# A planner's costs, and the order of weights, in a two-layer hybrid decoder trunk on one core

## The chip, the cores and the metric

The kernel runs on one core of a Trainium2 chip. The metric is the device time of one execution in microseconds. Before the change the median of three runs is 1481.27 us (1480.85 to 1481.48).

## What is computed

Two layers work on a sequence of 512 tokens of width 1024. All four branches of a layer read one projection of the same input; their gated outputs are projected, merged and projected again:

```python
for l in range(DEPTH):
    h = x @ w_in[l]
    (rw_p, rw_g, q_lat, kv_lat, k_pe, mla_g, conv_u, conv_g, xq, xg,
     merge) = jnp.split(h, SPLIT_POINTS, axis=-1)
    y_rwkv = _rwkv7_branch(rw_p, rw_g, ...)          # 8 heads x 64, delta-rule state, token by token
    y_mla = _mla_branch(q_lat, kv_lat, k_pe, mla_g, ...)   # causal softmax attention, 8 heads
    y_conv = _conformer_conv_branch(conv_u, conv_g, ...)   # val * sigmoid(glu), causal conv of width 31
    y_mem = _memory_xattn_branch(xq, xg, mem, ...)   # 4 heads into 256 memory tokens
    branches = jnp.stack([y_rwkv, y_mla, y_conv, y_mem], axis=2)
    proj = jnp.einsum('bsnc,ncd->bsnd', branches, w_o_branch[l])
    gates = jax.nn.sigmoid(merge.reshape(B, S, N_BRANCH, D) + b_gate[l])
    merged = jnp.sum(gates * proj, axis=2)
    out = merged @ w_out[l]
    x = _layer_norm(DEEPNORM_ALPHA * x + out, ln_g[l], ln_b[l])
```

## The kernel before

**Tiling.** The input is kept transposed (channels on partitions, 512 tokens along the row). Each f32 operand is split into two parts, `h` and `l` (ACT casts the first, DVE subtracts to get the second), and each product is three matmuls: `xl*wh`, `xh*wh`, `xh*wl`. A chunk of 128 output channels takes one weight DMA of 512 KB, the two halves of its split, and 24 matmuls of 512 columns. The names in the rows follow the work: `glu` and `val` are the convolution's chunks, `taps` its 31 multiply-adds on DVE (`cacc`), `mk` and `mv` the keys and values of the memory, `m` and `po` the merge gates and the output projections, `rg`, `mg`, `cg`, `xg` the gate paths. A last digit is the layer.

**Causal attention** (`pair_item`, L1492, and `mla_block`). Head pair, head and query block number a block: `ms013_0` are the scores of pair 0, head 1, block 3, layer 0. A block goes through PE (`ms`), DVE (mask and maximum `nmm`), ACT (exponential `mP` and its sum `smm`), DVE (reciprocal, scaling), PE (transposes `mt`) and ACT (copy `mPT`). At most three blocks are under way. When a pair's eight blocks are done, twenty matmuls (`mo`) make its output. `xhead` (L1265) does the same for the memory: `xs`, `xP`, `xt`, `xPTh`/`xPTl`, `xo`. `key_rotary` (L1373) turns the rotary part of the keys, and sends it by eight DMAs (`kTh`, `kTl`) to the partitions where the heads expect it.

**The recurrence** (`rwkv_unit`, L770) is done in chunks of 64 tokens, in units named layer, pair of head groups and half (`1_2_1` is the last). Its products are small: 64x64 tiles of PE. `bo`, `tk`, `w`, `yb` and `ty` are its bonus sums, transposes to tokens, state products, outputs and transposes back. `others` (L989) masks and copies two products out of one PSUM tile: `BP` on DVE, `RA` on ACT.

**The order.** All five engines run their instructions in program order. That order is made when the program is written, by a planner (`Plan`, L67). It keeps a clock for each engine and a time for each tile. `Engine.__getattr__` (L211) gives each ACT, DVE and POOL instruction a cost by its length, `start` adds latencies between engines (130 ns from one engine to another, 185 from PE, 220 to PE), and `run` (L149) takes the next step of whichever generator's time has come, or else the next matmul of the stream of weight items. `due` and `plan.t += ...` set back a generator's next step. `Space` (L242) hands out PSUM slots: three pools hold two, two and four banks. A weight item is picked when its condition holds, and its DMA is then put on SyncE's queue (SP), in the order in which items are picked; three weight slots (L30) hold what has been fetched. `conv_items` (L1235) has the conditions: `val0` may be picked once `L["glus"]` exceeds 0, and `glus` is counted in `glu`, when the projection has been computed.

All ACT, DVE and POOL instructions are recorded at L237, matmuls at L288, transposes at L293, DMAs at L300.

## Time and profile before

| | before |
|---|---|
| median of three runs | 1481.27 us |
| profiled execution | 1481.47 us |
| its span | 1479.7 us |
| granted TensorE clock | 0.999 |
| PE busy | 1465.4 us, 11751 matmuls |
| DVE busy | 1034.6 us |
| ACT busy | 682.7 us |
| POOL busy | 140.6 us |
| HBM traffic | 134.32 MB read, 5.77 MB written |

The profiled execution is longer than its span by 1.8 us, which lie before the first and after the last instruction. A busy time is the sum of an engine's instructions with overlaps counted once. A row of the timeline begins with the start and the length in microseconds, then has the engine, the line, the operation, the output and inputs, the shape and the count. What stands in brackets is idle time of the engine ahead of the row and what ended it.

### The profile page before, as it was taken

The numbers are of one execution on the slowest core, as the hardware profiler recorded it, in microseconds if no ns is written. First come the engines' busy times: TensorE is split into PE (matmuls) and PEld (weight loads), VectorE is DVE, ScalarE is ACT, GpSimd is POOL, SyncE is SP. The second block draws the span as 40 slices with busy tenths as digits, with TensorE's granted clock in tenths as the row PEclk, the third lists the DMA queues.
The fourth block names the chain that finished last, engine by engine and source line by source line (L and its number), as shares of the span: only waits on it lengthen the run. The fifth ranks groups of instructions, "written<-read, shape, count | busy, mean of one in ns | idle before, by whom it ended". The sixth has DMA issues, their size and how long they took to land.

```text
span 1479.7 us, 28903 instructions
## 1 busy us (share of the span) xinstructions
PE 1465.4 (99%) x11751; PEld 1230.6 (83%) x11751; DVE 1034.6 (70%) x2018; ACT 682.7 (46%) x1327; POOL 140.6 (10%) x329
## 2 busy tenths in 40 slices
PE   9999999999999999999999999999999999999997
PEld 8888888888888888888999888888888788888886
DVE  6799998765747575545564889987856475756747
ACT  5546653425354453443264466633454454444331
POOL 0000000030303020000010000000041103121002
PEclk9999999999999999999999999999999999999999
DMA  6444232232232323333353252433232323233522
GB/s 216 139 131 109 82 115 96 90 77 95 71 87 79 93 75 97 115 116 130 113 165 111 74 147 73 121 94 103 82 96 76 96 61 96 74 98 117 169 94 78
DMA packets 89157, 153.49 MB, mean 104 GB/s; under 512 B 41024, under 2 KB 47424, under 8 KB 89024
## 3 DMA queue, kind: packets, MB, share of 16 engines
q1 hardware_dynamic: 89024, 151.65, 34.1%
q8 instruction: 92, 1.51, 0.4%
q14 instruction: 41, 0.34, 0.1%
HBM read 134.32 MB, written 5.77 MB: 95 GB/s over the span
## 4 chain that ended last, share of the span: by engine, by line
PE 91%; DVE 3%; ACT 2%; DMA 2%; issue 0%; POOL 0%; SPq 0%; ACTq 0%; DVEq 0%; POOLq 0%
PE ps_m L288 24%; PE po L288 12%; PE ps_v L288 3%; PE ps_cg L288 3%; PE ps_rg L288 3%; PE ps_xg L288 3%; PE ps_k L288 3%; PE ps_mg L288 3%; PE ps_r L288 3%; PE ps_xq L288 3%; PE ps_val L288 3%; PE ps_glu L288 3%; PE pz L288 2%; PE ms L288 2%; PE x L288 2%; PE ps_mk L288 1%
## 5 line engine op out<-in xcount | busy, mean ns | idle before, releaser
L237 DVE SCALAR_TENSOR_TENSOR cacc<-hpad,prm,cacc 128x512 f32<-128x512 f32 x240 | 179.2, 749 | 4.0
L237 ACT ACTIVATE tm<-ps_m,prm 128x512 f32<-128x512 f32 x64 | 44.1, 689 | 151.4 <-PE ps_m L288 148.6
L237 DVE SCALAR_TENSOR_TENSOR mt<-tm,po 128x512 f32<-128x512 f32 x48 | 32.9, 686 | 85.9 <-PE po L288 85.8
L237 POOL TENSOR_TENSOR tmpW<-ZT,W 64x14 f32<-64x14 f32 (+6 forms) x112 | 42.7, 382 | 8.0
L237 ACT ACTIVATE mP<-ms,nmm 128x128 f32<-128x128 f32 (+3 forms) x64 | 33.8, 530 | 17.4 <-DVE nmm L237 11.4
L237 POOL TENSOR_TENSOR ZT<-ZT,tmpW 64x14 f32<-64x14 f32 (+6 forms) x112 | 39.6, 354 | 8.8
L237 POOL TENSOR_SCALAR ZT<-W 64x256 f32<-64x256 f32 x8 | 5.2, 649 | 368.3 <-DMA W<-scr 250.1
L237 DVE TENSOR_TENSOR merged<-merged,mt 128x512 f32<-128x512 f32 x48 | 33.4, 696 | 1.6
L237 ACT COPY mPT<-mt 128x128 f32<-128x128 f32 (+3 forms) x64 | 26.1, 428 | 17.0 <-PE mt L293 16.7
L237 POOL MEMSET D<- 128x8 f32 x8 | 0.9, 112 | 326.8 <-PE ms L288 310.1
L237 DVE CUSTOM_DVE_ANT_0 ms<-ms,causal 128x128 f32<-128x128 f32 (+3 forms) x64 | 31.0, 499 | 0.2
L293 PE MATMUL mt<-cst,mP 128*128 128x128 f32 x160 | 26.3, 274 | 1.5 <-DVE smx L237 1.0
L237 POOL TENSOR_SCALAR lrs<-lmv 128x1 f32<-128x1 f32 x8 | 4.0, 502 | 246.1 <-DVE lmv L237 241.1
L237 DVE TENSOR_SCALAR mP<-mP,smm 128x128 f32<-128x128 f32 (+3 forms) x64 | 24.8, 387 | 2.4
L237 DVE SCALAR_TENSOR_TENSOR merged<-tm,po 128x512 f32<-128x512 f32 x16 | 11.0, 687 | 21.5 <-PE po L288 21.5
L293 PEld LDWEIGHTS mt<-cst,mP 128*128 128x128 f32 x160 | 19.6, 140 | 7.2 <-ACT xP L237 1.4
L237 POOL TENSOR_SCALAR gr<-gm 128x8 f32<-128x8 f32 x8 | 1.6, 198 | 227.9 <-DVE gm L237 227.9
L237 ACT ACTIVATE yb<-yb,mr,gr 128x64 f32<-128x64 f32 x64 | 22.1, 430 | 1.1 <-DVE mr L237 1.1
L237 ACT ACTIVATE xP<-xs,nmx 128x256 f32<-128x256 f32 x32 | 15.2, 475 | 13.1 <-DVE nmx L237 8.1
L237 ACT ACTIVATE z<-z,lnb,lrs 128x256 f32<-128x256 f32 (+2 forms) x11 | 7.0, 666 | 30.7 <-DVE lnb L237 30.7
L288 PE MATMUL ms<-kTl,qT 96*128 96x128 f32 (+3 forms) x64 | 21.1, 330 | 0.0
L288 PE MATMUL ms<-kTh,qT 96*128 96x128 f32 (+3 forms) x64 | 20.6, 322 | 0.0
(3570 smaller groups left out, 5231.5 us busy)
## 6 DMA issues: line engine op xcount, KB each, us to landing
w<-in_w_ch_dram SPq DMA_DIRECT2D x146, 512.0 KB, 3.6
w<-in_w_o_dram SPq DMA_DIRECT2D x32, 512.0 KB, 3.5
w<-in_w_out_dram SPq DMA_DIRECT2D x16, 512.0 KB, 3.5
w<-in_w_lat_dram SPq DMA_DIRECT2D x15, 336.0 KB, 3.0
w<-in_w_mk_dram SPq DMA_DIRECT2D x8, 512.0 KB, 3.4
w<-in_w_mv_dram SPq DMA_DIRECT2D x8, 512.0 KB, 3.7
w<-in_w_qk_dram SPq DMA_DIRECT2D x8, 320.0 KB, 3.1
x<-in_xT_dram SPq DMA_DIRECT2D x8, 256.0 KB, 4.6
```

The source lines that it names most:

```text
L237: return self.plan.keep(f(*a, **k))
L288: plan.keep(nc.tensor.matmul(o, lhsT, rhs, start=start, stop=stop))
L293: plan.keep(nc.tensor.transpose(o, i, ident))
```

## The change

It changes costs and conditions of the planner, and with them the order; every engine has the same instructions as before.

- Tiles in PSUM of the tags `ps` and `pp` get an entry in `Plan.read`: a reader on another engine starts at least 130 ns after the last reader.
- An ACT instruction that also writes a sum (`accum_out`) costs 130 ns more, and a DVE reciprocal `90 + 4n` in place of `65 + 1.04n` (n is 1 to 8).
- `others` copies `RA` before `BP` if ACT's clock is behind DVE's.
- In layer 0 `glus` is counted when `glu` is picked, not when it has been computed; `val` can so be picked right behind it.
- The generator of the key transfers is set back by 4000 ns.

```diff
     def start(self, eng, outs, ins):
...
+        for n in ins:
+            t, e = self.read.get(n, (0.0, eng))
+            s = max(s, t + (130.0 if e != eng else 0.0))
...
     def end(self, eng, t, outs, ins):
...
+        for n in ins:
+            if n in self.read:
+                self.read[n] = t, eng
...
-                c = 65 + 0.83 * n + 120 * hasattr(k.get("scale"), "tensor") + 90 * hasattr(k.get("bias"), "tensor")
+                c = 65 + 0.83 * n + 120 * hasattr(k.get("scale"), "tensor") + 90 * hasattr(k.get("bias"), "tensor") + 130 * ("accum_out" in k)
...
+            elif name == "reciprocal":
+                c = 90 + 4 * n
...
+        if tag in ("ps", "pp"):
+            self.plan.read[t.tensor.name] = 0.0, ""
...
+                first = plan.clk["ACT"] < plan.clk["DVE"]
+                if first:
+                    right()
                 for s in SUB:
                     V.tensor_tensor(out=by2(BP[s])[:, :, :, 64:128], in0=y0[:, 0, s],
                                     in1=cc("minc").unsqueeze(1).unsqueeze(1).to_broadcast([128, 2, 2, 64]), op=ALU.mult)
-                for s in SUB:
-                    S.copy(by2(RA[s])[:, :, :, 64:128], y0[:, 1, s].rearrange("p h c w -> p c h w"))
+                if not first:
+                    right()
...
-                L["glus"] += 1
+                L["glus"] += l
...
+            def first():
+                if l == 0:
+                    L["glus"] += 1
+
+            ch_item(CH_U + 4 + i, f"glu{i}", glu, lambda: L["vals"] >= i - l and (i < 2 or L["taps"][i - 2] >= 20), first)
...
             plan.due(*kr)
+            plan.t += 4000.0
             yield
```

What this moves is seen in the order of the instructions. First SyncE's queue in layer 0, around the first key transfers; `w8` is glu0's weight in both. Before, `w9` and `w10` are mk0 and mk1, `w11` is val0, `w12` mk2:

```order
L300 DMA w8_464<-in_w_ch_dram 128x1024
L300 DMA w9_494<-in_w_mk_dram 128x1024
L300 DMA w10_537<-in_w_mk_dram 128x1024
L300 DMA kTh0_0_356<-krh_0_580 32x512
L300 DMA kTl0_0_357<-krl_0_581 32x512
L300 DMA w11_609<-in_w_ch_dram 128x1024
L300 DMA kTh1_0_358<-krh_0_580 32x512
```

With the change `w9` is val0, `w10` and `w11` are mk0 and mk1, `w12` is glu1:

```order
L311 DMA w8_464<-in_w_ch_dram 128x1024
L311 DMA w9_494<-in_w_ch_dram 128x1024
L311 DMA w10_537<-in_w_mk_dram 128x1024
L311 DMA w11_603<-in_w_mk_dram 128x1024
L311 DMA kTh0_0_356<-krh_0_583 32x512
L311 DMA kTl0_0_357<-krl_0_584 32x512
L311 DMA w12_649<-in_w_ch_dram 128x1024
```

val0's weight has moved from fourth to second place, and the first key transfers stand behind one more weight. On PE val0 follows glu0 with the change; before, it followed mk1.

Next PE and DVE in the first head pair of layer 0, from the scores ms100 to the first products of `mo0`. PE before:

```order
L288 MATMUL ms100_0_1521<-kTh2_0_360,qTl10_0_1207 128x128
L293 MATMUL mt003_0_1529<-cst_81,mP003_0_1479 128x128 x4
L288 MATMUL ps_val2_0_1390<-xl7_0_247,w27h_1345 128x512
L288 MATMUL ps_val2_0_1390<-xh7_0_246,w27h_1345 128x512
L288 MATMUL ps_val2_0_1390<-xh7_0_246,w27l_1346 128x512
L288 MATMUL ms110_0_1543<-kTl3_0_363,qT11_0_1208 128x128
L288 MATMUL ms110_0_1543<-kTh3_0_362,qT11_0_1208 128x128
L288 MATMUL ms110_0_1543<-kTh3_0_362,qTl11_0_1209 128x128
L293 MATMUL xt01_0_1531<-cst_81,xP00_0_1317 128x128 x2
L293 MATMUL xt01_0_1531<-cst_81,xP01_0_1421 128x128 x2
L293 MATMUL mt013_0_1565<-cst_81,mP013_0_1499 128x128 x4
L293 MATMUL mt100_0_1573<-cst_81,mP100_0_1538 128x128
```

PE with the change:

```order
L299 MATMUL ms100_0_1524<-kTh2_0_360,qTl10_0_1207 128x128
L304 MATMUL mt003_0_1529<-cst_81,mP003_0_1480 128x128 x4
L299 MATMUL ms110_0_1546<-kTl3_0_363,qT11_0_1208 128x128
L299 MATMUL ms110_0_1546<-kTh3_0_362,qT11_0_1208 128x128
L299 MATMUL ms110_0_1546<-kTh3_0_362,qTl11_0_1209 128x128
L304 MATMUL mt013_0_1557<-cst_81,mP013_0_1501 128x128 x4
L299 MATMUL ms101_0_1565<-kTl2_0_361,qT10_0_1206 128x256
L299 MATMUL ms101_0_1565<-kTh2_0_360,qT10_0_1206 128x256
L299 MATMUL ms101_0_1565<-kTh2_0_360,qTl10_0_1207 128x256
L304 MATMUL xt01_0_1544<-cst_81,xP00_0_1317 128x128 x2
L304 MATMUL xt01_0_1544<-cst_81,xP01_0_1424 128x128 x2
L299 MATMUL mo0_0_1247<-mPT000_0_1395,v0_0_928 64x128
```

The last three val2 matmuls stand ahead of ms100 now, xt01 stands behind mt013, and mt100 no longer follows mt013: its place is behind the twenty matmuls of `mo0`, which begin in the last row. DVE in the same blocks, from the reciprocal of block 003 to the scaling of block 013, before:

```order
L237 RECIPROCAL smm003_0_1481<-smm003_0_1481 128x1
L237 TENSOR_SCALAR mP003_0_1479<-mP003_0_1479,smm003_0_1481 128x512
L237 SCALAR_TENSOR_TENSOR cacc1_0_1050<-hpad1_113,prm0_227,cacc1_0_1050 128x512
L237 TENSOR_TENSOR xPTl00_0_1516<-xt00_0_1497,xPTh00_0_1515 128x512
L237 RECIPROCAL smm013_0_1501<-smm013_0_1501 128x1
L237 TENSOR_SCALAR mP013_0_1499<-mP013_0_1499,smm013_0_1501 128x512
```

and with the change:

```order
L246 RECIPROCAL smm003_0_1482<-smm003_0_1482 128x1
L246 TENSOR_SCALAR mP003_0_1480<-mP003_0_1480,smm003_0_1482 128x512
L246 SCALAR_TENSOR_TENSOR hpad0_112<-tglu2_0_1159,ps_val2_0_1388 128x512
L246 RECIPROCAL smm013_0_1503<-smm013_0_1503 128x1
L246 TENSOR_SCALAR mP013_0_1501<-mP013_0_1501,smm013_0_1503 128x512
```

Between the two scalings hpad0, which reads val2's PSUM tile, stands in place of a tap of the convolution and xPTl00.

Last PE in the second head pair of layer 0, ahead of mt113. Before:

```order
L288 MATMUL ps_xq2_0_1746<-xh3_0_193,w29l_1662 128x512
L288 MATMUL ps_xq2_0_1746<-xl4_0_211,w29h_1661 128x512
L288 MATMUL ps_xq2_0_1746<-xh4_0_210,w29h_1661 128x512
L288 MATMUL ps_xq2_0_1746<-xh4_0_210,w29l_1662 128x512
L293 MATMUL mt113_0_1833<-cst_81,mP113_0_1796 128x128 x4
L288 MATMUL ps_xq2_0_1746<-xl5_0_224,w29h_1661 128x512
```

With the change:

```order
L299 MATMUL ps_xq2_0_1783<-xh3_0_193,w29h_1645 128x512
L299 MATMUL ps_xq2_0_1783<-xh3_0_193,w29l_1646 128x512
L304 MATMUL mt103_0_1809<-cst_81,mP103_0_1752 128x128 x4
L299 MATMUL ps_xq2_0_1783<-xl4_0_211,w29h_1645 128x512
L299 MATMUL ps_xq2_0_1783<-xh4_0_210,w29h_1645 128x512
L299 MATMUL ps_xq2_0_1783<-xh4_0_210,w29l_1646 128x512
L304 MATMUL mt113_0_1828<-cst_81,mP113_0_1775 128x128 x4
L299 MATMUL ps_xq2_0_1783<-xl5_0_224,w29h_1645 128x512
```

Three more matmuls of xq2 and the transposes mt103 stand between the first twelve of xq2 and mt113. xq2 as a whole has moved too: before, its first three matmuls follow pk2; with the change mt102, ms103, mt112, ms113 and xs11 stand between pk2 and xq2.

In the last unit of layer 1 the state products w1 and w2 and the transposes ty_1_2_1 come later by six, nine and three matmuls of 512 columns, and the outputs yb follow the transposes ty_1_2_0 directly, where nine matmuls stood between. From the merge's po00 on, some 107 us before the end, PE's order is as before.

More of the change, by code (lines that the diff above doesn't have):

```diff
@@ L89, in __init__ @@
         self.slots = {}
+        self.read = {}
     def start(self, eng, outs, ins):
@@ L991, in others, with right @@
                 yield
+                def right():
+                    for s in SUB:
+                        S.copy(by2(RA[s])[:, :, :, 64:128], y0[:, 1, s].rearrange("p h c w -> p c h w"))
+                first = plan.clk["ACT"] < plan.clk["DVE"]
+                if first:
+                    right()
                 for s in SUB:
@@ L1247, in val @@
                 L["vals"] += 1
-            ch_item(CH_U + 4 + i, f"glu{i}", glu, lambda: L["vals"] >= i - l and (i < 2 or L["taps"][i - 2] >= 20))
+            def first():
+                if l == 0:
+                    L["glus"] += 1
+            ch_item(CH_U + 4 + i, f"glu{i}", glu, lambda: L["vals"] >= i - l and (i < 2 or L["taps"][i - 2] >= 20), first)
             ch_item(CH_U + i, f"val{i}", val, lambda: PRM[l] is not None and L["glus"] > i and (i < 2 or L["taps"][i - 2] == 30))
```

## The prediction

> **What bounds the kernel now.** First the page: the busy time of each engine, the clock granted to TensorE (PE) in forty slices, and the chain that ended last.

> ```profile
> PE 1465.4 (99%) x11751; PEld 1230.6 (83%) x11751; DVE 1034.6 (70%) x2018; ACT 682.7 (46%) x1327; POOL 140.6 (10%) x329
> PEclk9999999999999999999999999999999999999999
> PE 91%; DVE 3%; ACT 2%; DMA 2%; issue 0%; POOL 0%; SPq 0%; ACTq 0%; DVEq 0%; POOLq 0%
> ```

> PE is busy 99% of the span at full clock, and nine tenths of the chain is PE itself. A change that only reorders the same instructions can therefore win no more than PE's waits, and lose only by making new ones. So I next asked for busy time by stretch. The columns are the stretch and its length, then the busy time of PE, weight loads, DVE, ACT and POOL.

> ```profile
> 40.00:200.00 160.00, 157.38 (x939) 133.89 (x938) 142.82 (x304) 90.48 (x201) 2.07 (x3) 1.00 0.43 122
> 200.00:1440.00 1240.00, 1239.08 (x10428) 1034.85 (x10427) 837.97 (x1589) 561.97 (x1067) 127.21 (x299) 1.00 0.33 99
> 1440.00:1480.00 40.00, 31.01 (x160) 26.48 (x158) 30.02 (x73) 6.29 (x12) 10.16 (x16) 0.95 0.23 79
> ```

> From 200 to 1440 us PE lacks 0.92 us of 1240. From 40 to 200 us (projections, softmax of both attentions) it lacks 2.62. The last 40 us lack 8.99, but there the order of PE is not changed. Next the list of PE's waits: who waited, for whom, total, times, longest.

> ```profile
> PE mt L293 <- DVE smx L237: 1.0, 1, 1.0
> PE w L288 <- ACT yc L237: 0.6, 1, 0.6
> PE mt L293 <- DVE mP L237: 0.5, 1, 0.5
> PE ps_val L288 <- DVE w11l L237: 0.5, 1, 0.5
> PE ps_xq L288 <- ACT xql L237: 0.4, 1, 0.4
> ```

> Each happens once, so each can be looked up. Busy time understates them, since a pipelined matmul's end is drawn into the wait. I therefore price a wait as the distance between two starts less the usual distance. Usual is 0.23 us for 512 columns, as the rows below show.

> **The change part by part.** Nothing is added or taken away on any engine, and the number of changes of PE's tile shape is the same. Every term is a wait that goes or comes.

> *Weights of val0.* The order on SyncE's queue changes, and val0's weights now come second instead of fourth. Starts on PE, then the queue:

> ```profile
> 41.38 0.28 PE L288 MATMUL ps_mk<-meml,w9h 128*128 128x256 f32 x1
> ...
> 47.33 0.29 PE L288 MATMUL ps_mk<-memh,w10h 128*128 128x256 f32 x1
> 47.46 0.28 PE L288 MATMUL ps_mk<-memh,w10l 128*128 128x256 f32 x1
> 47.90 0.50 PE L288 MATMUL ps_val<-xl,w11h 128*128 128x512 f32 x1 [0.17 <-ACT w11h L237]
> 48.24 0.40 PE L288 MATMUL ps_val<-xh,w11h 128*128 128x512 f32 x1
> 49.16 0.50 PE L288 MATMUL ps_val<-xh,w11l 128*128 128x512 f32 x1 [0.53 <-DVE w11l L237]
> ```

> ```profile
> 26.97 6.67 SPq L300 DMA_DIRECT2D w<-in_w_mk_dram  x2
> 42.40 0.53 SPq L300 DMA_DIRECT2D w<-in_w_ch_dram  x1
> ```

> From 47.46 to 47.90 is 0.44 where 0.13 is usual (47.33 to 47.46): 0.31 lost. From 48.24 to 49.16 is 0.92 for 0.23: 0.69 lost. Both wait for the two halves of w11, whose DMA was issued only at 42.40, behind two key transfers, which wait for the rotated key. In the new order val0 uses the weight issued second. That issue lies in the 26.97 row (two DMAs, over at 33.64), and val0 now stands where the 41.38 row has mk0, right behind glu0, so its weight has some 8 us to land and be split. Gain 1.00. The key transfers themselves move behind one more weight and land in the same few microseconds. I cost them at nothing: all of val0, mk0 and mk1, 24 matmuls each, stand ahead of the first scores, which read the keys. Without that cover the price would again be at most the 1.00.

> *mt100, mt013.* Each of the 64 causal score blocks goes PE ms, DVE max, ACT exponential with its sum, DVE reciprocal and scaling, PE transposes mt. The planner now reckons 130 ns more for the sum and more for the reciprocal, so it sets other work between.

> ```profile
> 131.38 0.62 PE L293 MATMUL xt<-cst,xP 128*128 128x128 f32 x4
> 131.84 0.60 PE L293 MATMUL mt<-cst,mP 128*128 128x128 f32 x4
> 132.97 0.30 PE L293 MATMUL mt<-cst,mP 128*128 128x128 f32 x1 [0.53 <-DVE mP L237]
> ```

> Four transposes take as long as xt01's four (131.38 to 131.84, 0.46), but mt100 starts 1.13 after mt013: 0.67 lost. Now mt100 stands behind all twenty matmuls of mo0. Gain 0.67. In exchange mt013 has lost distance to its own scores:

> ```profile
> 126.79 0.40 PE L288 MATMUL ms<-kTl,qT 96*128 96x512 f32 x1
> 127.49 0.40 PE L288 MATMUL ps_val<-xl,w27h 128*128 128x512 f32 x1
> 128.20 0.60 PE L293 MATMUL xt<-cst,xP 128*128 128x128 f32 x4
> 128.88 0.47 PE L288 MATMUL ps_val<-xl,w27h 128*128 128x512 f32 x1
> ```

> ```profile
> 130.73 0.15 DVE L237 RECIPROCAL smm<-smm 128x1 f32<-128x1 f32 x1
> 130.92 0.49 DVE L237 TENSOR_SCALAR mP<-mP,smm 128x512 f32<-128x512 f32 x1
> 131.53 0.68 DVE L237 SCALAR_TENSOR_TENSOR hpad<-tglu,ps_val 128x512 f32<-128x512 f32 x1
> ```

> From ms013 at 126.79 to mt013 at 131.84 were 5.05 us. Three val2 matmuls (127.49 to 128.20, 0.71) and xt01 (0.46) no longer stand between, so 3.88 are left. The scaling of mP013 ended at 130.92 + 0.49 = 131.41, 4.62 behind ms013. DVE's order between has changed too: a cacc and an xPTl are gone, and hpad0 stands there instead. It reads val2, whose last group starts now after ms013 (0.70), val2 (0.71), xt00 and mt012 (128.20 to 128.88, 0.68). It has three matmuls of 0.23, with the end of the last some 0.2 later: 2.98 behind ms013. With hpad0 (0.68), and 0.68 for reciprocal and scaling by the starts 130.73 and 130.92, mP013 is ready at 4.34. A new wait of about 0.5. Its bounds are 0, if DVE is ahead, and 4.62 - 3.88 = 0.74, if DVE does as before. I take 0.5, since hpad0's release is worked out from rows.

> *xq2 and mt113.*

> ```profile
> 144.03 0.39 PE L288 MATMUL pk<-lth,w28l 128*128 128x512 f32 x1
> 144.83 0.50 PE L288 MATMUL ps_xq<-xl,w29h 128*128 128x512 f32 x1 [0.41 <-ACT xql L237]
> ...
> 150.67 0.39 PE L288 MATMUL ps_xq<-xh,w29l 128*128 128x512 f32 x1
> 152.04 0.63 PE L293 MATMUL mt<-cst,mP 128*128 128x128 f32 x4 [0.98 <-DVE smx L237]
> ```

> xq2 starts 0.80 after the last pk2 matmul where 0.23 is usual: 0.57 lost to ACT's xql, which had to empty a PSUM tile. In the new order xq2 stands behind ms103, ms113, xs11 and two groups of transposes. The two scores alone are six matmuls of 0.23, 1.4 us. Gain 0.57. mt113 starts 1.37 after the matmul ahead of it: 1.14 lost. Three more matmuls of xq2 (0.69) and the four transposes of mt103 (0.46) now stand ahead of it behind ms113, 1.15 together. On DVE a split of w30 now precedes ms113's maximum instead of following it, while the queue ahead starts earlier. I take a gain of 1.04, with bounds 0 (the split is felt in full) and 1.14.

> *xq3 of layer 1.*

> ```profile
> 867.45 0.39 PE L288 MATMUL pk<-lth,w146l 128*128 128x512 f32 x1
> 867.96 0.50 PE L288 MATMUL ps_xq<-xl,w147h 128*128 128x512 f32 x1
> ```

> ```profile
> 866.34 0.62 ACT L237 CAST yxg0h<-xy 128x512 fp32r<-128x512 f32 x1
> ```

> The distance 0.51 is 0.28 over the usual; xq3 waits for ACT's xql. Of ACT's queue the cast of yxg0 shown is moved away from before it, and its 0.62 exceed the wait. Gain 0.28.

> *The rest.* The wait of w3 of unit 1_0_0 for yc (listed, 0.6) keeps its order and stays, and so does po13's for tm13. The earlier place of the RA copies on ACT, longer sums in the norms, and the later bonus and token steps of units 0_0_0, 1_0_0 and 1_2_0 touch steps for which PE does not wait in the list. They bring nothing, and cost nothing while rows from 200 us on lack 0.92 of 1240. But 32 causal and 16 memory softmax groups of layer 1 are shuffled as well. I set 0.3 us for new waits there, between 0 and 2 us: none, or four of the size that the list shows for mP (0.5); 0.3 is near the lower end, as no layer 1 softmax wait is among the listed ones.

> *The last unit.* The order of its state products changes: w1, w2, the transposes ty and the outputs yb are each later or next to each other.

> ```profile
> 1342.77 0.39 PE L288 MATMUL ps_rg<-xh,w214l 128*128 128x512 f32 x1
> 1343.09 0.45 PE L288 MATMUL w<-S,Gs 64*64 64x64 f32 x8
> 1343.47 0.50 PE L288 MATMUL ps_rg<-xl,w215h 128*128 128x512 f32 x1
> 1343.81 0.39 PE L288 MATMUL ps_rg<-xh,w215h 128*128 128x512 f32 x1
> ```

> The eight 64x64 products start 0.32 after the last 512-column matmul (0.23 usual), and the second matmul behind them 0.34 after the first: a detour to small tiles costs 0.09 + 0.11 = 0.20. [...] But w0, w1, w2 and yb are four detours in either order, so the order gives 0, and I take 0; with one saved, the sum would come out 0.2 lower. PE has no listed wait in this unit, so nothing is to be won by moving; to be lost is a wait for yb or ty, which have some tenths of a microsecond to spare.

> **Sum.** 1.00 + 0.67 + 0.57 + 1.04 + 0.28 = 3.56 goes, 0.5 + 0.3 = 0.8 comes: 2.8 us less. The profiled execution took 1481.47, 0.20 above the median of the runs shown (1481.27) and within their spread. 1481.47 - 2.8 = 1478.7, from the median 1478.5. I predict 1478.6.

> **Rivals.** *DVE keeps the gain.* Between 40 and 200 us DVE works 142.82 of 160, 89%, and nearly all removed waits lie there. If PE arrives earlier but DVE cannot, the next transposes wait instead. Against it: waits were single, and before each DVE had free time. From two fifths to all of the gain of 2.8 would come back: 1479.8 to 1481.5.

> *More goes.* No new wait at all, mt113 whole (0.1 more), and the list's wait of w3 and po13's shrink by some 0.9 because everything ahead shifts: 3.56 + 1.0 = 4.6, 1476.9. For it: the planner's costs come nearer to the rows. Against it: their order is unchanged.

> *Slower.* The planner believes softmax sums longer and so puts another 512-column DVE step (hpad0 above, 0.68) ahead of a reciprocal whose transposes come soon. That costs 0.5 at mt013. Repeated at more than 7 of the 64 blocks (3.56 / 0.5) the kernel is slower than before, at 14 by over 0.2%: with 16, 1481.47 - 3.56 + 8 = 1485.9. Against it: most mt groups stand as far behind their scores as before, or farther.

> *It does not do what it says.* In the last unit there is no wait to remove, and the same number of detours. If yb or ty then comes late by 0.5, the result is 1479.1, inside my forecast's range.

> **How the numbers follow.** The forecast (1477.8 to 1479.8, the last rival included) has 0.53, DVE keeps the gain 0.25, more goes 0.16, slower 0.06. About 0.2% (2.96 us) is what a measurement of this kernel can tell from no change, so the border is at 1478.3 below and 1484.2 above. The forecast lies across the lower one: 0.21 of its 0.53 falls below. Faster is 0.21 + 0.16 = 0.37; slower 0.05, of the 0.06; the rest, 0.58, is the same. Leaving out the slower case and the outer ends, the range is 1476.6 to 1481.4. Its lower end is 1481.27 less the 3.56, mt113's 0.1 and 1.0 of the waits that I let stand.

> **What would show it.** In the new list of PE's waits, ps_val, ps_xq and the smx wait of mt should be gone, and mt with mP should remain once, near 131 us, for hpad0. val0 should begin straight after glu0 near 41.4. The window 40 to 200 should lack about 0.6 in place of 2.62, and 200 to 1440 about 1. The clock row and the last 40 us should not move. I am wrong if several new mt waits stand in layer 1 (815 to 970 us), if val1 or mk1 now waits for a late weight, or if yb waits in the last unit.

## The result, and the profile after

| | before | after |
|---|---|---|
| median, 13 runs each on one chip | 1481.27 us (1480.61 to 1482.01) | 1477.88 us (1477.14 to 1478.25) |
| profiled execution | 1481.47 us | 1477.30 us |
| its span | 1479.7 us | 1475.5 us |

The ratio is 0.9977, with a 95% interval from 0.9968 to 0.9985: 3.39 us faster, where 2.8 were forecast. The predicted 1478.6 is 0.7 too high. Before's time beside each experiment is from the same chip as the experiment (1481.05 to 1481.29).

Lines have moved in the changed kernel: ACT, DVE and POOL record at L246 (L237 before), matmuls at L299 (L288), transposes at L304 (L293), DMAs at L311 (L300). The page after, busy time, granted clock and the head of the chain:

```profile
PE 1464.9 (99%) x11751; PEld 1232.1 (84%) x11751; DVE 1034.8 (70%) x2018; ACT 681.8 (46%) x1327; POOL 144.8 (10%) x329
PEclk9999999999999999999999999999999999999999
PE 96%; DVE 1%; ACT 1%; POOL 0%; issue 0%; POOLq 0%
```

Work and clock are the same, and PE's share of the chain has risen from 91% to 96%: what has gone is waiting. By stretch (stretch, length, then busy time of PE, weight loads, DVE, ACT, POOL):

```profile
0.00:40.00 40.00, 38.74 (x231) 36.73 (x232) 24.20 (x54) 24.45 (x54) 1.15 (x11) 1.00 0.65 214
40.00:200.00 160.00, 159.57 (x956) 136.97 (x955) 145.10 (x312) 91.25 (x201) 2.06 (x3) 1.00 0.44 120
200.00:1440.00 1240.00, 1239.68 (x10427) 1035.36 (x10426) 837.18 (x1583) 560.10 (x1064) 131.43 (x299) 1.00 0.33 99
1440.00:1475.50 35.50, 26.89 (x142) 23.07 (x140) 28.34 (x70) 5.98 (x11) 10.15 (x16) 0.94 0.20 71
```

and the first stretch of before:

```profile
0.00:40.00 40.00, 37.90 (x229) 35.40 (x230) 23.79 (x54) 23.91 (x51) 1.16 (x11) 1.00 0.61 201
```

From 40 to 200 us PE now lacks 0.43 (2.62 before; some 0.6 was forecast), from 200 to 1440 us 0.32 (0.92; about 1 was forecast). The end is unchanged: before, the 39.7 us to the span's end lacked 8.69, now the 35.5 us lack 8.61. The first 40 us lack 0.84 less, but that isn't the change's: up to glu0 at 35 us PE's order is that of before, and in the executions below PE waits near 7 us between nothing and 1.05 us for the casts of its first input, and up to 0.4 for glu0 at 35 us. Without it the profiled executions differ by 4.17 - 0.84 = 3.3 us, close to the medians' 3.39.

The list of PE's waits after the change, whole (who waited, for whom, total, times, longest):

```profile
PE warm L299 <- POOL reset L246: 1.3, 1, 1.3
PE mt L304 <- ACT mPT L246: 0.4, 1, 0.4
PE po L299 <- ACT tm L246: 0.2, 1, 0.2
```

Of the five waits that the prediction quoted none is left under its name; one wait of mt is there, with ACT's copy named as what ended it. `warm` is ahead of the first product, in both kernels.

### The profile page after: what moved, and what is told of

Same layout as the page of the kernel before. It is cut to its first block, busy times and chain, and to the rows that moved or that the text cites. A ratio compares the mean times of both kernels' runs of the same rounds, so it can differ in the third digit from the quotient of the medians.

```text
span 1475.5 us, 28902 instructions
## 1 busy us (share of the span) xinstructions
PE 1464.9 (99%) x11751; PEld 1232.1 (84%) x11751; DVE 1034.8 (70%) x2018; ACT 681.8 (46%) x1327; POOL 144.8 (10%) x329
## 4 chain that ended last, share of the span: by engine, by line
PE 96%; DVE 1%; ACT 1%; POOL 0%; issue 0%; POOLq 0%
PE ps_m L299 24%; PE po L299 12%; PE ps_v L299 3%; PE ps_cg L299 3%; PE ps_rg L299 3%; PE ps_xg L299 3%; PE ps_xq L299 3%; PE ps_mg L299 3%; PE ps_k L299 3%; PE ps_val L299 3%; PE ps_glu L299 3%; PE ps_r L299 3%; PE pz L299 2%; PE ms L299 2%; PE pl L299 2%; PE x L299 2%
## 5 line engine op out<-in xcount | busy, mean ns | idle before, releaser
L246 DVE SCALAR_TENSOR_TENSOR cacc<-hpad,prm,cacc 128x512 f32<-128x512 f32 x240 | 179.1, 749 | 3.9
L246 ACT ACTIVATE tm<-ps_m,prm 128x512 f32<-128x512 f32 x64 | 44.1, 688 | 149.6 <-PE ps_m L299 146.9
L246 DVE SCALAR_TENSOR_TENSOR mt<-tm,po 128x512 f32<-128x512 f32 x48 | 33.0, 687 | 91.3 <-PE po L299 91.3
L246 POOL TENSOR_TENSOR tmpW<-ZT,W 64x14 f32<-64x14 f32 (+6 forms) x112 | 43.4, 388 | 8.0
L246 ACT ACTIVATE mP<-ms,nmm 128x128 f32<-128x128 f32 (+3 forms) x64 | 33.7, 529 | 20.6 <-DVE nmm L246 15.7
L246 POOL TENSOR_TENSOR ZT<-ZT,tmpW 64x14 f32<-64x14 f32 (+6 forms) x112 | 39.8, 355 | 8.8
L246 POOL TENSOR_SCALAR ZT<-W 64x256 f32<-64x256 f32 x8 | 4.7, 587 | 361.5 <-DMA W<-scr 361.5
L246 DVE TENSOR_TENSOR merged<-merged,mt 128x512 f32<-128x512 f32 x48 | 33.3, 694 | 1.6
L246 POOL MEMSET D<- 128x8 f32 x8 | 0.9, 111 | 329.6 <-PE ms L299 313.7
L246 DVE CUSTOM_DVE_ANT_0 ms<-ms,causal 128x128 f32<-128x128 f32 (+3 forms) x64 | 31.2, 499 | 0.6 <-PE ms L299 0.3
L246 ACT COPY mPT<-mt 128x128 f32<-128x128 f32 (+3 forms) x64 | 26.4, 428 | 5.3 <-PE mt L304 5.0
L246 POOL TENSOR_SCALAR lrs<-lmv 128x1 f32<-128x1 f32 x8 | 4.0, 501 | 244.7 <-DVE lmv L246 239.7
L304 PE MATMUL mt<-cst,mP 128*128 128x128 f32 x160 | 26.9, 274 | 0.4 <-ACT mPT L246 0.4
L246 DVE TENSOR_SCALAR mP<-mP,smm 128x128 f32<-128x128 f32 (+3 forms) x64 | 24.8, 387 | 2.4
L246 DVE SCALAR_TENSOR_TENSOR merged<-tm,po 128x512 f32<-128x512 f32 x16 | 11.0, 687 | 22.0 <-PE po L299 19.9
L304 PEld LDWEIGHTS mt<-cst,mP 128*128 128x128 f32 x160 | 20.2, 140 | 6.8 <-issue 0.8
L246 POOL TENSOR_SCALAR gr<-gm 128x8 f32<-128x8 f32 x8 | 3.3, 409 | 225.7 <-DVE gm L246 225.7
L246 ACT ACTIVATE yb<-yb,mr,gr 128x64 f32<-128x64 f32 x64 | 22.1, 431 | 0.7 <-DVE mr L246 0.7
L299 PE MATMUL ms<-kTl,qT 96*128 96x128 f32 (+3 forms) x64 | 21.5, 337 | 0.0
L246 ACT ACTIVATE z<-z,lnb,lrs 128x256 f32<-128x256 f32 (+2 forms) x11 | 7.0, 666 | 30.6 <-DVE lnb L246 30.6
L299 PE MATMUL ms<-kTh,qTl 96*128 96x128 f32 (+3 forms) x64 | 20.6, 323 | 0.0
L299 PE MATMUL ms<-kTh,qT 96*128 96x128 f32 (+3 forms) x64 | 20.6, 322 | 0.0
```

Of the source, the lines that this page charges most:

```text
L246: return self.plan.keep(f(*a, **k))
L299: plan.keep(nc.tensor.matmul(o, lhsT, rhs, start=start, stop=stop))
L304: plan.keep(nc.tensor.transpose(o, i, ident))
```

## The experiments

The theory behind the prediction: the time is PE's work and its waits, each wait can be read from the order with the durations of before's trace, and the longer costs of sums and reciprocals are what moves the softmax steps to better places. The main rivals: DVE keeps the gain, and the costs do it by no truth of theirs. Waits in the text are start to start less the usual distance, as in the prediction; the lists show idle time, which is mostly shorter.

**val0 early, alone.** Before, with two parts of the change only:

```diff
-                L["glus"] += 1
+                L["glus"] += l
...
+            ch_item(CH_U + 4 + i, f"glu{i}", glu, lambda: L["vals"] >= i - l and (i < 2 or L["taps"][i - 2] >= 20), first)
...
+            plan.t += 4000.0
```

> The kernel before with only the count of glu at its picking and the set-back of the key transfers, no cost changed. Theory A (each wait is a price of its own, removed by its own part): the two waits for w11's halves go, 1.00 us, every other wait of before stays: about 1480.3 where before is 1481.3. Rival B (DVE keeps the gain): PE comes 1.0 us earlier to the softmax stretch and waits there longer, so mt100 and mt113 wait about 1.0 more together and the time stays within 0.2 of before.

Measured: 1479.66 us against 1481.05, ratio 0.9990 [0.9981, 0.9999]. The list of PE's waits:

```profile
PE mt L293 <- DVE smx L237: 1.0, 1, 1.0
PE mt L293 <- DVE mP L237: 0.6, 1, 0.6
PE w L288 <- ACT yc L237: 0.6, 1, 0.6
PE ps_xq L288 <- ACT xql L237: 0.4, 1, 0.4
```

The two waits for w11 (0.31 + 0.69) are gone, and all others stand as before. The gain of 1.4 us is the 1.00 within its interval. Theory A held; rival B, by which DVE takes the gain back, fell, since no wait grew by more than 0.05.

**The costs, alone.** Before, with the longer sum and reciprocal only:

```diff
+ 130 * ("accum_out" in k)
...
+            elif name == "reciprocal":
+                c = 90 + 4 * n
```

> The kernel before with only the longer costs of sums and reciprocals. Theory A (the softmax waits mt100 0.69, mt113 1.14 and the xq2 and xq3 waits 0.57 and 0.29 are there since the planner took softmax for shorter than it is): they go or shrink, w11's stay: 1478.6 to 1479.6. Rival C (the turn-taking moved them): all of them stay, within 0.5 of before.

Measured: 1488.07 us against 1481.05, ratio 1.0044 [1.0031, 1.0057]: slower by 7.0. The waits of mt113 (1.13) and xq2 (0.56) are still there, and new ones have come: 1.50 and 0.81 of mt near 130 us, two of some 0.5, and a large one in layer 1. PE and then DVE there:

```profile
893.32 0.79 PE L290 MATMUL ps_glu<-xh,w149l 128*128 128x512 f32 x1 [2.32 <-DVE w149l L239]
893.91 0.63 PE L290 MATMUL ps_glu<-xl,w149h 128*128 128x512 f32 x1
894.34 0.63 PE L290 MATMUL ps_glu<-xh,w149h 128*128 128x512 f32 x1
```

```profile
891.44 0.69 DVE L239 SCALAR_TENSOR_TENSOR xg<-txg,ps_xg 128x512 f32<-128x512 f32 x1 [1.58 <-ACT txg L239]
892.04 1.22 DVE L239 TENSOR_TENSOR w149l<-w,w149h 128x1024 fp32r<-128x1024 f32 x1
```

The split of w149 was ready to run (ACT's cast of w149h was over at 889.30), but in DVE's order it stands behind xg, which waits 1.58 for ACT. PE loses 2.48 and then runs at half pace: 0.43 between starts (893.91 to 894.34) where 0.23 is usual. What theory A expected of the costs fell, and C with it: by themselves they make the kernel slower, not faster.

**The turns, alone.** Before, with `Plan.read` only:

```diff
+            t, e = self.read.get(n, (0.0, eng))
+            s = max(s, t + (130.0 if e != eng else 0.0))
```

> The kernel before with only the rule that engines take turns on one PSUM tile. Theory A (the softmax waits hang on the costs): mt100, mt113 and w11's waits stay; the waits for ACT's copies and reads out of PSUM (xq2 0.57, xq3 0.29, w3 0.65) may go: 1479.8 to 1481. Rival C (the turn-taking moved the softmax): mt100 and mt113 go, 1479.0 or less.

Measured: 1484.02 us against 1481.05, ratio 1.0017 [1.0008, 1.0026]: slower by 3.0. Three of the list's rows:

```profile
PE ps_val L297 <- DVE w11l L244: 1.8, 1, 1.8
PE mt L302 <- DVE mP L244: 1.4, 1, 1.4
...
PE mt L302 <- DVE smm L244: 0.7, 1, 0.7
```

The waits of mt113, xq2 and xq3 are gone here, without any change of cost. But val0, still behind mk1, now waits longer for w11 (1.94), and two waits of mt (1.50 and 0.85) have come near 133 us; behind them the granted clock falls to a half for 3.4 us (last section). Neither theory held whole: mt113's wait went, as C has it, and the time rose.

**Without RA first.** After, with `RA` always copied behind `BP`:

```diff
-                first = plan.clk["ACT"] < plan.clk["DVE"]
-                if first:
-                    right()
...
-                if not first:
-                    right()
+                for s in SUB:
+                    S.copy(by2(RA[s])[:, :, :, 64:128], y0[:, 1, s].rearrange("p h c w -> p c h w"))
```

> The changed kernel with BP always ahead of RA, all else as changed; PE and DVE move in 28 and 3 places only, ACT in none. Theory D (w3's wait of 0.65 went because ACT copies RA ahead of DVE's BP, and so reaches yc0 earlier): it comes back, about 1478.5 where the changed kernel is 1477.9. Rival E (it went because PE and ACT meet differently there for other reasons): no wait at w3, 1477.9 within 0.3.

Measured: 1478.12 us, ratio 0.9979 [0.9970, 0.9988]; the change whole has 0.9977, so the times don't tell the two apart. The rows do. In unit 1_0_0 first before, ACT and then the state product w3 on PE:

```profile
1175.84 0.65 ACT L237 COPY RA<-x_1x 128x256 f32<-128x256 f32 x2 [3.70 <-DVE BP L237]
...
1177.32 0.79 ACT L237 ACTIVATE yc<-cb,prm 128x512 f32<-128x512 f32 x1
```

```profile
1178.16 0.45 PE L288 MATMUL w<-S,Gs 64*64 64x64 f32 x8 [0.57 <-ACT yc L237]
```

then after:

```profile
1168.35 0.70 ACT L246 COPY RA<-x_1x 128x256 f32<-128x256 f32 x2
1171.62 1.06 ACT L246 CAST w194h<-w 128x1024 fp32r<-128x1024 f32 x1 [2.58 <-DMA w<-in_w_o_dram]
1172.65 0.78 ACT L246 ACTIVATE yc<-cb,prm 128x512 f32<-128x512 f32 x1
```

```profile
1173.88 0.45 PE L299 MATMUL w<-S,Gs 64*64 64x64 f32 x8
```

and in the experiment:

```profile
1171.92 0.65 ACT L246 COPY RA<-x_1x 128x256 f32<-128x256 f32 x2 [3.69 <-DVE BP L246]
...
1173.40 0.79 ACT L246 ACTIVATE yc<-cb,prm 128x512 f32<-128x512 f32 x1
```

```profile
1174.24 0.45 PE L299 MATMUL w<-S,Gs 64*64 64x64 f32 x8 [0.76 <-ACT yc L246]
```

RA and BP come out of one PSUM tile, x_1x in the rows. In before RA is second: ACT stands idle for 3.70 us until DVE's BP is over (1175.75; RA starts at 1175.84), the cast and yc queue behind RA, and w3 waits for yc. After, RA is first: it starts at 1168.35 without a wait, the cast waits only for its weight (2.58), and w3 has no wait in the rows. Theory D held in the rows: with this edit alone taken out of the change, w3's wait is back. ACT's order is the same with the edit and without it; what the edit turns round is which of the two engines waits for the other. By the traces ACT's RA stands idle for BP eight times in before, 11.4 us together, and once after, for 0.4 us; DVE's BP stands idle for RA never in before, and three times after, 1.8 us together. Made on the kernel of before alone, the edit changes no instruction's place on any engine, but by the program ACT's RA would be ahead of BP in seven of the eight units. That kernel was not run, so what the edit is worth there is not shown. In before and in this run the second of the two reads starts 0.09 us after the end of the first, and being the second cost ACT 3.70 and 3.69 us; what makes it wait was not shown.

**Without the turns.** After, with `Plan.read` taken out (the lines of the third experiment removed).

> The changed kernel without the rule of turns on a PSUM tile; costs, val0 early and RA first stay. Theory F (the parts add up: what the turns alone took away, mt113 1.14, xq2 0.54 and xq3 0.28, comes back when they are taken out): those three waits stand in the list, about 1479.8. Rival G (the order of the crowded stretch is dealt anew by every change of a cost, so that parts do not add up): other waits than these three, the time anywhere from 1478 to 1486.

Measured: 1480.76 us against 1481.29, ratio 0.9996 [0.9987, 1.0005]. mt113 (1.14) and xq2 (0.54) wait as before, mt twice near 130 us (0.96 and 0.69), and tk at 1083.5 us (0.51). Three of these make one row of the list:

```profile
PE mt L295 <- DVE mP L239: 2.3, 3, 1.0
```

F held for two of its three waits (that of xq3 stayed away) and not for the rest: three others came, as G has it, and the time is 1.0 above F's.

**Without the costs.** After, with the old costs of sum and reciprocal.

> The changed kernel without the longer costs of sums and reciprocals; turns, val0 early and RA first stay. Theory F: what the turns alone showed without its waits for w11 (2.2) and w3 (0.9): the two mt waits near 133 us of 1.5 and 0.85 stay, about 1480.8. Rival G: other waits. A rival H (with val0 early the costs do nothing more): 1477.9, no mt wait.

Measured: 1479.34 us, ratio 0.9988 [0.9979, 0.9997]. The list:

```profile
PE mt L302 <- DVE smx L244: 1.0, 1, 1.0
...
PE mt L302 <- DVE mP L244: 0.6, 1, 0.6
PE ps_xq L297 <- ACT xql L244: 0.4, 1, 0.4
```

These are before's waits less those for w11 and w3, each at its old size: mt113 1.14, mt100 0.74, xq2 0.55, xq3 0.28. H fell, and the waits of mt that F has were not there; G's "other waits" is what is left. The turns, which alone took away mt113's, xq2's and xq3's waits, take away none of them here: the same edit, on an order that has val0 early and RA first, moves other instructions.

**val0 late.** After, with `glus` counted in `glu` again and without the 4000 ns.

> The changed kernel without val0 early and without the set-back of the key transfers; turns, costs and RA first stay. Theory F: w11's waits of 1.0 come back and nothing else, about 1478.9. Rival G: mt and ps_val waits in layer 0 of another size, 1480 or more.

Measured: 1487.64 us against 1481.29, ratio 1.0040 [1.0027, 1.0053]: 9.8 us above the change whole, where only 1.3 hangs on w11l itself. Three of its rows:

```profile
PE ps_glu L299 <- DVE w149l L246: 2.3, 1, 2.3
PE xt L304 <- DVE xP L246: 1.9, 1, 1.9
...
PE ps_val L299 <- DVE w11l L246: 1.1, 1, 1.1
```

F fell, and the time is as G has it, but the two largest waits are not those that G named: 2.09 of xt at 170.75 us, and 2.48 of glu in layer 1. An edit at 40 us deals the order anew up to 895 us, where DVE's w149l is late again as in the run with the costs alone.

**The costs as the rows have them.** In the change's trace the read of a sum takes ACT 0.19 to 0.23 us and the reciprocal DVE 0.16. If better costs made the better order, these should be no worse than 130 and 94:

```diff
-  ... + 130 * ("accum_out" in k)
+  ... + 200 * ("accum_out" in k)
...
-                c = 90 + 4 * n
+                c = 155 + 1.04 * n
```

> The changed kernel with a sum at 200 ns more (in place of 130) and a reciprocal at 156 ns, as the rows of the trace have them. Theory I (nearer costs make fewer waits): the wait of mt013 (0.60) goes too and none comes, 1477.3 or less. Rival G (every change of a cost deals the order anew): new waits, 1479 to 1485.

Measured: 1490.56 us, ratio 1.0061 [1.0048, 1.0073], the second slowest of all. PE waits 3.70 for a key transfer of layer 1, 1.78 and 0.93 for w22 near 95 us:

```profile
872.73 0.44 PE L299 MATMUL ms<-kTl,qT 96*128 96x128 f32 x1 [3.54 <-DMA kTl<-xkl]
```

I fell. New waits came, as G has it, but the time is 5.6 above G's upper end.

This settles less than it seems to, for 200 and 156 ns are lengths of instructions, and the planner's other costs are nearer to the distance from one start to the next: a cast of 1024 columns costs 915 ns in the planner, takes 1044 ns in the rows of the change, and stands 945 ns ahead of the next start (medians). By that measure a sum costs 0.09 us (its read starts at 128.27, the next instruction at 128.36; 92 ns is the median of 72), and the reciprocal 0.19 (129.62 to 129.81 below). A sum near 92 ns together with a reciprocal near 190 was not tried.

**hpad0 later.** After, with hpad0 of val2 (layer 0) put off by 600 ns in the planner's time, so that it leaves the place ahead of mt013's scaling:

```diff
+                def put():
+                    plan.t += 600.0 if (l, i) == (0, 2) else 0.0
+                    if (l, i) == (0, 2):
+                        yield
                     V.scalar_tensor_tensor(out=hpad[:, 30:542], in0=d["t"], scalar=1.0, in1=ps, op0=ALU.add, op1=ALU.mult)
```

> The changed kernel with hpad0 of val2 in layer 0 put 600 ns later by the planner; on DVE it then stands behind the scaling of block 013, a tap of the convolution in its old place. Theory J (mt013 waits 0.60 since DVE does hpad0, which itself waits for val2, ahead of the scaling): the wait of mt013 is gone or under 0.2, 1477.3. Rival K (mt013 waits for ACT's copy to empty its PSUM tile, as the list names it): it stays at 0.5 or more, 1477.9.

Measured: 1477.56 us against 1481.14, ratio 0.9976 [0.9967, 0.9985]. First the change whole, PE (ms013, then mt013) and DVE:

```profile
125.95 0.40 PE L299 MATMUL ms<-kTl,qT 96*128 96x512 f32 x1
...
129.73 0.27 PE L299 MATMUL ms<-kTh,qTl 96*128 96x128 f32 x1
130.44 0.63 PE L304 MATMUL mt<-cst,mP 128*128 128x128 f32 x4 [0.43 <-ACT mPT L246]
```

```profile
129.01 0.69 DVE L246 SCALAR_TENSOR_TENSOR hpad<-tglu,ps_val 128x512 f32<-128x512 f32 x1 [0.82 <-PE ps_val L299]
129.62 0.16 DVE L246 RECIPROCAL smm<-smm 128x1 f32<-128x1 f32 x1
129.81 0.49 DVE L246 TENSOR_SCALAR mP<-mP,smm 128x512 f32<-128x512 f32 x1
```

then the experiment, PE (mt003 and mt013 in one row) and DVE:

```profile
129.09 1.13 PE L304 MATMUL mt<-cst,mP 128*128 128x128 f32 x8
```

```profile
128.96 0.49 DVE L246 TENSOR_SCALAR mP<-mP,smm 128x512 f32<-128x512 f32 x1
...
130.17 0.68 DVE L246 SCALAR_TENSOR_TENSOR hpad<-tglu,ps_val 128x512 f32<-128x512 f32 x1
```

With hpad0 behind the scaling, mt013 goes without a gap, though ACT's copy, which the list names, starts as late as it did (129.75): theory J, that DVE holds mt013, held. The time is that of the change all the same, for 0.89 came at tk, 1080 us, and 0.45 at pq, 138.5 us.

**Other costs of a sum.** The change with 150, 100 and 160 ns in place of 130:

> The changed kernel with the sum at 150 ns in place of 130: 62 places on PE move. Theory G (each deal of the order has its own waits, with no regard to which cost is nearer): one or two waits other than those of the changed kernel, 1477 to 1480. Theory I (nearer costs, fewer waits): 1477.9 or less.

> The changed kernel with the sum at 100 ns in place of 130 (387 places on PE move). Theory G: between 1477 and 1486, its waits in the stretches 100 to 200 or 800 to 1000 us. Theory I: slower by a little, mt113's wait partly back, 1478 to 1479.

> The changed kernel with the sum at 160 ns (1298 places on PE move). Theory G: like the measured costs, a large deal with a large wait somewhere, 1480 to 1490, its waits in the softmax stretches. Theory I: 1477.9 or less.

Measured, against 1481.14: 150 gives 1477.80, ratio 0.9978 [0.9969, 0.9987]; 100 gives 1482.35, 1.0010 [1.0001, 1.0019]; 160 gives 1491.23, 1.0069 [1.0056, 1.0081]. By PE's order 62, 387 and 1298 instructions stand elsewhere than in the change. With 160 the list begins:

```profile
PE po L299 <- DVE yrg2l L246: 3.1, 1, 3.1
...
PE x L299 <- ACT PT L246: 1.9, 1, 1.9
```

Ten nanoseconds more in a cost of the planner (160 against 150) make 13 us on the chip, where every engine does the same instructions. At 150 both theories have the time; at 100 and 160 I fell. G has the time at 100; at 160 it is 1.2 above G's, and the two largest waits lie at 1192 and 1383 us, outside the softmax stretches that G named. There is no slope toward either measure of a sum: 100, the nearest to 0.09 us, loses a little; 130 and 150 win; 160 and, with the longer reciprocal, 200 lose most.

## Why the prediction was right, and where it was not

**The sum did not add up by edit, but it did by wait.** Against before, val0 early alone gives -1.4 us, the costs +7.0 and the turns +3.0: +8.6 together, where the whole gives -3.4. RA first was not run alone; the 0.65 that the rows tie to it would not close that gap. Taken out of the whole, the turns are worth 2.9 us, the costs 1.5, val0 early 9.8 and RA first 0.2. The forecast came out because it priced no edit. It went through the order that the whole change makes and asked at each wait of before what stands there now.

- *val0, 1.00:* right. val0 starts straight behind glu0, at 41.13 (41.4 was forecast), and neither val1 nor mk1 waits for its weight. The experiment with this part alone shows it by itself.
- *mt100, 0.67, and xq2, 0.57:* right. Both waits are gone from rows and list.
- *mt113, 1.04:* gone whole, 1.14. It starts 0.24 behind the matmul ahead of it:

```profile
148.46 0.40 PE L299 MATMUL ps_xq<-xh,w29l 128*128 128x512 f32 x1
148.70 0.60 PE L304 MATMUL mt<-cst,mP 128*128 128x128 f32 x4
```

- *xq3 of layer 1, 0.28:* right; the list has it no more.
- *mt013, a new wait of 0.5:* right in place and cause, 0.60 in size. The working put the end of mP013's scaling 4.34 behind ms013; the rows above have 129.81 + 0.49 - 125.95 = 4.35. The wait is longer by the time from DVE's end to PE's start (130.30 to 130.44), which the working left out. The list's name for the releaser, ACT's mPT, was not the one that held it.
- *"The wait of w3 of unit 1_0_0 for yc ... keeps its order and stays":* **wrong**, and this is the step that failed. The order of ACT there has indeed not changed; the working took that to mean that the wait had not. But RA now runs ahead of BP instead of waiting for it, in several microseconds that were ACT's idle time, and no longer holds the cast and yc. It brought 0.65. "They bring nothing" was said of the RA copies in general; for this unit it was wrong. po13's wait, 0.36, did stay.
- *The rest, 0.3 for new waits in layer 1:* none came.
- *The last unit, 0:* right; no wait of ty or yb is listed, and the end lacks what it lacked.

Worked out anew with these sizes: 1.00 + 0.67 + 0.57 + 1.14 + 0.28 + 0.65 - 0.60 = 3.71 less. Medians say 3.39 with about 1.3 either way, and the profiled executions without the first 40 us 3.3; some 0.3 is smaller than what could be traced.

**The cause that the prediction gave for the softmax part fell.** It said that the planner reckons more for sum and reciprocal "so it sets other work between". The costs alone leave mt113 and xq2 waiting and add waits of 1.50 and 2.48 us; costs set to the lengths in the rows give the second slowest kernel; and turns without costs take the three waits away on the kernel of before, but not with val0 early and RA first. mt113 and xq2 wait together or not at all: both in each of the four kernels without the turns, neither in seven of the ten with them, both in the other three (no costs, a sum of 100, a sum of 160). So the turns were needed in all that was tried, and don't suffice. What is shown is that, among the combinations tried, mt113, xq2 and xq3 all lose their waits without a new one above 0.9 us only in this one and its near variants (without RA first, hpad0 later, a sum of 150). Why the planner arrives at it isn't a matter of one cost: each edit shifts its clocks, and every later choice follows. In before, and in the losing versions but for that with 160, most of the waiting lies in the two softmax stretches and the projections ahead of them (48 to 175 us, 870 to 900 us); in the first of these DVE too is busy most of the time, for 145.10 of the 160 us from 40 to 200 after the change.

**The slower rival** was put at 0.06, with hpad0-like steps repeated. In the change it did not happen. Its kind is not rare among the neighbours: of the eleven other versions that hold parts of the change or other sums, five were slower than before by over 0.15%, by late splits, key transfers and scalings: through a few waits of some 1.5 to 4 us rather than many of 0.5, and through the clock that fell behind them (last section). That second price stood nowhere in the prediction.

## What to carry to other kernels

Where a planner deals the order and the bound engine is 99% busy, price the order that comes out and not the edit that made it: list the few waits, and for each compare what stands between producer and consumer on both engines, before and after, the idle queue of the producer's engine included. Where two engines read one tile, look also at which waits for which: in unit 1_0_0 that turned round, and ACT's 3.70 us of standing idle for BP went, with ACT's order the same. Don't let waits pile up close together: each of the eight falls of the clock inside the kernel in these runs came behind 3.41 us in which PE was idle for 1.77 or more. Don't read a gain as proof that a cost is truer, and don't expect the parts to add up; build the neighbours (each cost a little off, each part left out), look through their orders for splits and transfers that came late, and time a few.

## What the runs showed of the hardware

```profile
46.30:49.71 3.41, 1.95 (x13) 1.27 (x11) 1.60 (x2) 1.90 (x3) 0.00 (x0) 1.00 0.60 192
49.71:53.12 3.41, 3.08 (x15) 2.57 (x16) 2.11 (x4) 2.33 (x3) 0.00 (x0) 1.00 0.48 159
131.63:135.04 3.41, 1.64 (x13) 1.32 (x12) 3.18 (x11) 1.67 (x7) 0.00 (x0) 1.00 0.03 5
135.04:138.45 3.41, 3.12 (x27) 2.93 (x29) 3.25 (x10) 1.53 (x5) 0.00 (x0) 0.50 0.00 0
```

The longer wait lies across the border of two windows, and the clock stays. The two shorter ones, 1.50 and 0.85, lie almost wholly in one, and the clock falls at its end. In the eight windows ahead of a fall PE is busy for 0.33 to 1.64 us; the least busy windows behind which the clock stays have 1.76 (1465.63 to 1469.04 us of the run with a sum of 150) and 1.95, the first row above. So what counted in these traces is the idle time in one window, not the length of one wait: about half a window, 1.77 us of it, went with a fall in the run with the turns alone, where 1.46 and 0.33 in the two windows around the longer wait did not, nor did the 1.65 of the run with a sum of 150. In the run with val0 late the clock holds for 1.3 us of work after the wait of 2.09 at 170.75 us: it falls at 172.03, where that window ends.

In seven of the eight cases the clock is back after one window. Behind the 3.70 us wait of the run with the lengths as costs it stays at 0.50 for three (871.67 to 881.91 us), though PE is busy for 2.35, 3.11 and 3.41 us of them; what kept it down is open. In the run with the costs alone PE works 2.9 us at half the clock behind its 2.48 us wait; an estimate from that is some 1.5 us more lost. This is part of why the losing versions lose more than their lists of waits add up to. By these traces waits that add up to 1.8 us within 3.41 have to be counted as a risk in this kernel, and whether they cost depended on where the windows lay.

**Being second at a PSUM tile** cost ACT 3.70 us of standing still in unit 1_0_0 of before (3.69 without RA first), which nothing in PE's list but a 0.6 us wait two steps later (0.8 without RA first) gave away.
